# Token products in parts of 512, 512 and 128 instead of three of 384, in a hybrid encoder layer on one core

## The chip, the cores and the metric

One NeuronCore of a Trainium2 chip runs the whole step in one launch. The metric is device microseconds from the start to the end of an execution, as a median of several.

## The reference, cut to what matters

One inference step of one encoder layer with 1024 prompt tokens and 8 samples of 16 tokens (1152 tokens in all), model width 1024, everything in fp32:

```
z   = x @ w_in                     # 80 column tiles of 128, and 16 gate columns
o_A = chunk-band softmax attention (16 heads of 64; own chunk of 64 and 8 chunks before it)
o_B = gated DeltaNet (causal conv of 4, SiLU, delta rule by chunks, 8 heads of 128)
o_C = cross-attention into 256 memory tokens (4 heads of 256)
h   = LayerNorm(alpha * x + (sum_b sigmoid(gate_b) * o_b) @ w_out)
y   = LayerNorm(alpha * h + relu(h @ w_ff1 + b_ff1)^2 @ w_ff2 + b_ff2)
```

The outputs are y for prompt and samples, the new caches of keys and values of A and of the memory, and the states of the convolution and of the delta rule.

## The kernel before

Every wide product is made of three products in fp32r: each operand is split into a high and a low part, and high by high, high by low and low by high are added up in PSUM. `gemm` (line 183) walks the eight blocks of 128 input features. In each it issues three products, with `whi`, `whi` and `wlo` as the stationary operand and tokens as the moving one. Each product brings its own weight load.

A *unit* here is one tile of 128 output features over all 1152 tokens. `projected` (line 195) makes a unit in three parts of `CW` = 384 tokens. A part takes 24 products into one PSUM tile of the pair `ps` (tag g, two tiles), and is then handed to an evacuation function. The 1024 prompt tokens end 256 tokens into the third part; its last 128 tokens are the samples. There are 80 units of `w_in`, 32 of the first feed-forward matrix (line 1258), and a narrow one of 64 output columns for the gates of B (line 523).

The order of the stages is: A (attention, with the front of B woven in), C, B, output projection, feed-forward. In stage A, for each group g of two heads, the code makes q, k and v (`a_qk`, `a_v`), eight `a_prompt` units, `a_sample`, a gate unit and the three convolution units of `b_front`. A scheduler places the instructions on the queues of the engines by priorities and its own model. Each engine takes its queue strictly in order. DMAs are issued from the queue of SyncE (loads) and that of ScalarE (stores), in the same order as the other work there.

The tile `y` (two buffers of 384 columns in stage A) is shared: the evacuation of k copies a part of k into it and stores it (`o_akp`, lines 313 to 315, in the second and third part); the evacuation of v copies each part into it (line 338), stores it (`o_avp`) and lets TensorE transpose it (`pvt`); the convolution computes in it (lines 604 to 628), transposes it (`tp`) and stores it (`spq`, `spk`). A buffer is free again when its store has landed and its transposes are done.

`a_prompt` handles two query tiles of 128 against up to six key tiles. Four of them are used by both query tiles (256 moving columns). The two at the edges of the band are used by one query tile only; the other half of their 256 columns is zero, set once in `phase_a`.

`merge` (line 751) adds the gated branches up in DRAM (`og`), part by part. Stage B works on groups of three chunks of 128 tokens and keeps its 384.

Of the kernel before, what the change touches and what calls it, by code (L numbers as in the profile page):

```python
# [19 lines left out]
P = 128  # L20
D = 1024
SEQ = 1024
DB = 8
# [3 lines left out]
NCH = NT // CW  # L27
KT = D // P
# [35 lines left out]
class K:  # L64
# [158 lines left out]
    def load_x(self, pool):  # L223
        nc = self.nc
        xT = self.d["xT"].rearrange("c p (k n) -> c p k n", k=KT)
        self.first = [self.w_in(0)]
        for c in range(NCH):
            n = slice(c * CW, (c + 1) * CW)
            if c == 1:
                self.first.append(self.w_in(8))  # L230
            for k in range(KT):
                xr = pool.tile([P, (CW, 640, CW, 3 + CW)[k % 4]], F32, name=("e", "pt", "y", "z")[k % 4], bufs=2)[:, 0:CW]
                self.xlast = nc.sync.dma_start(xr, xT[c, :, k, :]).ins.name
                self.split(self.xh[:, k, n], self.xl[:, k, n], xr, "act")


    def phase_a(self, keep, pool, ps):
# [15 lines left out]
        for i in range(2):  # L253
            th = pool.tile([P, 6, 256], F32R, name=f"pth{i}")
            tl = pool.tile([P, 6, 256], F32R, name=f"ptl{i}")
            for t in (th, tl):
                nc.gpsimd.memset(t.bitcast(F32)[:, 4, 0:128], 0.0)
                nc.gpsimd.memset(t.bitcast(F32)[:, 5, 128:256], 0.0)
            A["pt"].append((th, tl))

        A["kl"] = [pool.tile([P, NT], F32R, name=f"kl{h}") for h in range(2)]
# [22 lines left out]
    def a_qk(self, g, pool):  # L284
        nc, d, A = self.nc, self.d, self.A

        qs = [pool.tile([P, NT], F32R, name=f"qs{h}") for h in range(2)]
        kd = [pool.tile([P, NT], F32R, name=f"kd{h}") for h in range(2)]
# [6 lines left out]
        def ev_q(c, p):  # L295
            n = slice(c * CW, (c + 1) * CW)
            for t, (r, o) in zip(qs, rows):
                nc.scalar.mul(t[r, n], p[r], 0.125)
                nc.vector.scalar_tensor_tensor(t[o, n], p[r], 0.125, t[r, n].bitcast(F32), op0=ALU.mult, op1=ALU.subtract)
            if c == 2:  # L300
                s = p[:, 256:384].rearrange("p (b i) -> p b i", b=DB)
                nc.scalar.mul(qb[0:64, :, 0:16], s[0:64], 0.125)
                nc.scalar.mul(qb[64:128, :, 16:32], s[64:128], 0.125)

        def ev_k(c, p):
            n = slice(c * CW, (c + 1) * CW)
# [4 lines left out]
            if c > 0:  # L311
                y = pool.tile([P, CW], F32, name="y", bufs=2)
                nc.scalar.copy(y, p)  # L313
                m = slice(128, 384) if c == 1 else slice(0, 256)
                nc.scalar.dma_start(d["o_akp"][g][:, (c - 1) * 256:c * 256], y[:, m])
            if c == 2:
                nc.gpsimd.tensor_copy(kr, y[:, 256:384])
# [11 lines left out]
    def a_v(self, g, pool, ps):  # L329
# [6 lines left out]
        def ev_v(c, p):  # L336
            vr = pool.tile([P, CW], F32, name="y", bufs=2)
            nc.scalar.copy(vr, p)
            if c == 1:
                nc.scalar.dma_start(d["o_avp"][g][:, 0:256], vr[:, 128:384])  # L340
            if c == 2:
                nc.scalar.dma_start(d["o_avp"][g][:, 256:512], vr[:, 0:256])
            pt = ps.tile([P, 512], F32, name="pvt", tag="f")
            for i in range(3):
                self.transpose(pt[:, i * P:(i + 1) * P], in_=vr[:, i * P:(i + 1) * P], identity=self.ident)
            m = 3 if c < 2 else 2
            src = pt[:, :m * P].rearrange("p (t h e) -> p t h e", t=m, h=2)
            dst = vv[:, 3 * c:3 * c + m]
            nc.scalar.copy(dst[:, :, :, 0:64], src)
            nc.vector.tensor_sub(dst[:, :, :, 64:128], src, dst[:, :, :, 0:64].bitcast(F32))  # L350
            if c == 2:
                nc.scalar.copy(vs, pt[:, 256:384])
# [20 lines left out]
    def a_prompt(self, g, G, h, pool, ps):  # L373
# [43 lines left out]
        e = 4 * 256 + P  # L417
        m = 256 if p0 >= 4 else P
        fh, fl = th.rearrange("p s q -> p (s q)"), tl.rearrange("p s q -> p (s q)")
        nc.scalar.copy(fh[:, e:e + m], tb[nb][:, :m])  # L420
        nc.vector.tensor_sub(fl[:, e:e + m], tb[nb][:, :m], fh[:, e:e + m].bitcast(F32))
# [76 lines left out]
    def b_setup(self, keep, pool, ps):  # L498
# [6 lines left out]
        z = pool.tile([P, CW], F32, name="e", bufs=2)  # L505
# [17 lines left out]
        for c in range(NCH):  # L523
            n = slice(c * CW, (c + 1) * CW)
            p = self.psg.tile([P, 512], F32, name="ps", tag="g")
            for k in range(KT):
                self.mm(p[0:64, :CW], lhsT=wh[:, k, :], rhs=self.xh[:, k, n], start=k == 0, stop=False)
                self.mm(p[0:64, :CW], lhsT=wh[:, k, :], rhs=self.xl[:, k, n], start=False, stop=False)
                self.mm(p[0:64, :CW], lhsT=wl[:, k, :], rhs=self.xh[:, k, n], start=False, stop=k == KT - 1)
            xa = pool.tile([P, CW], F32, name="e", bufs=2)[0:8]  # L530
            xb = pool.tile([P, CW], F32, name="e", bufs=2)[0:8]
            nc.scalar.activation(xa, p[0:8, :CW], AF.Identity, bias=par[:, 1:2])
# [7 lines left out]
            nc.scalar.activation(e, p[32:40, :CW], AF.Exp, scale=-1.0)  # L540
# [45 lines left out]
    def b_front(self, h, pool, ps):  # L586
# [3 lines left out]
        def conv(x, prev):  # L590
# [3 lines left out]
            def ev(c, p):  # L594
                n = slice(c * CW, (c + 1) * CW)
                z = pool.tile([P, 3 + CW], F32, name="z", bufs=2)
                nc.scalar.copy(z[:, 3:], p)
                if c == 0:
                    nc.gpsimd.memset(z[:, 0:3], 0.0)
                else:  # L600
                    nc.gpsimd.tensor_copy(z[:, 0:3], prev[0][:, CW:CW + 3])
                prev[0] = z
                y = pool.tile([P, CW], F32, name="y", bufs=2)
                nc.scalar.activation(y, p, AF.Copy, scale=wc[:, 3:4])  # L604
                w = CW if c < 2 else 256
                for i in range(3):
                    nc.vector.scalar_tensor_tensor(y[:, :w], z[:, i:i + w], wc[:, i:i + 1], y[:, :w], op0=ALU.mult, op1=ALU.add)  # L607
                if c == 2:
# [4 lines left out]
                    nc.gpsimd.tensor_copy(zs[:, :, 3:19], z[:, 259:387].rearrange("p (b i) -> p b i", b=DB))  # L613
                    ys = y[:, 256:384].rearrange("p (b i) -> p b i", b=DB)
# [3 lines left out]
                    nc.gpsimd.tensor_copy(co[:, 0, :], z[:, 256:259])  # L618
                    nc.gpsimd.tensor_copy(co[:, 1:9, :], zs[:, :, 16:19])
                    nc.scalar.dma_start(d["o_conv"][t], co.rearrange("p a i -> p (a i)"))  # L620
                e = pool.tile([P, CW], F32, name="e", bufs=2)
# [3 lines left out]
                for i in range(3):  # L625
                    self.transpose(tp[:, i * P:(i + 1) * P], in_=y[:, i * P:(i + 1) * P], identity=self.ident)
                if x < 2:
# [3 lines left out]
                    for i in range(3):  # L631
                        nc.scalar.activation(jk, tp[:, i * P:(i + 1) * P], AF.Square, accum_out=acc[:, h, 3 * c + i:3 * c + i + 1])
                if x > 0:
                    kn = pool.tile([P, CW], F32, name="kn", bufs=2)
                    nc.scalar.copy(kn, tp[:, :CW])
# [95 lines left out]
    def b_gate(self, a, t, pool, tags=("e", "oraw")):  # L731
# [4 lines left out]
        def ev(c, p):  # L736
            n = slice(c * CW, (c + 1) * CW)
            if a != 1:
                o = pool.tile([P, CW], F32, name=tags[1], bufs=2)
                nc.sync.dma_start(o, raw[t][:, n])  # L740
            e = pool.tile([P, CW], F32, name=tags[0], bufs=2)
# [3 lines left out]
            else:  # L745
                nc.vector.tensor_mul(e, e, o)
                self.merge(t, c, e, pool)
# [3 lines left out]
    def merge(self, t, c, e, pool):  # L751

        nc = self.nc
        dst = self.og[t][:, c * CW:(c + 1) * CW]
        if (t, c) in self.started:
            p = pool.tile([P, CW], F32, name="part", bufs=2)
            nc.sync.dma_start(p, dst)
            nc.gpsimd.tensor_add(e, e, p)
        self.started.add((t, c))
# [141 lines left out]
    def b_tail(self, h, c, pool, ps, o, gate, sample):  # L901
# [18 lines left out]
        self.merge(h, c, gate, pool)  # L920
# [121 lines left out]
    def c_q(self, h, pool):  # L1042
        nc, C = self.nc, self.C
        qh = pool.tile([P, 2, NT], F32R, name="qh", bufs=2)
        ql = pool.tile([P, 2, NT], F32R, name="ql", bufs=2)
        qz = C["qz"][h % 2]

        def ev_q(dt):
            def ev(c, p):
                n = slice(c * CW, (c + 1) * CW)  # L1050
                nc.scalar.mul(qh[:, dt, n], p, 0.0625)
                nc.vector.scalar_tensor_tensor(ql[:, dt, n], p, 0.0625, qh[:, dt, n].bitcast(F32), op0=ALU.mult, op1=ALU.subtract)
                if c == 2:
                    for a, b in self.spread2(qz[:, dt], p[:, 256:384]):
                        nc.scalar.mul(a, b, 0.0625)
# [127 lines left out]
    def out_early(self, po, pool):  # L1183
# [6 lines left out]
        for c in range(2):  # L1190
# [3 lines left out]
            for k in range(KT):  # L1194
                mg = pool.tile([P, CW], F32, name=("e", "oraw")[k % 2], bufs=2)
# [11 lines left out]
    def phase_out(self, pool, ps):  # L1207
# [36 lines left out]
        with self.pool("p2b") as pb:  # L1244
# [7 lines left out]
            for f0 in range(0, NF, blk):  # L1252
                hid = []
                for f in range(f0, f0 + blk):
# [3 lines left out]
                    for c in range(NCH):  # L1258
                        n = slice(c * CW, (c + 1) * CW)
# [145 lines left out]
```

## Time and profile before

| | |
|---|---|
| median of 3 runs | 2831.02 us (2816.75 to 2837.72) |
| profiled execution, whole | 2831.98 us |
| profiled execution, span from first to last instruction | 2830.2 us |
| mean granted clock of TensorE | 0.976 of full speed |
| TensorE products (PE), busy | 2685.3 us, 95% of the span, 16361 instructions |
| weight loads (PEld), busy | 2486.4 us, 88%, 16361 instructions |
| VectorE (DVE), busy | 1460.4 us, 52% |
| ScalarE (ACT), busy | 1008.4 us, 36% |
| GpSimd (POOL), busy | 819.5 us, 29% |

PE is the matmul side of TensorE, PEld its weight loads, which overlap. Products are pipelined: the duration of one is longer than the distance to the next, so the cost of a product in a stream is read from start to start, not from its duration. What lies outside the span is 1.8 us.

### The profile page before, as it was taken

How to read it: one execution, taken by the hardware profiler on the slowest of the kernel's cores; microseconds unless marked ns; L12 is line 12 of the kernel's file. 1: busy time of each engine (PE TensorE's matmuls, PEld its weight loads, DVE VectorE, ACT ScalarE, POOL GpSimd, SP SyncE). 2: the span in 40 equal slices, each digit the busy share in tenths (PEclk: the TensorE clock that was granted, in tenths of full speed). 3: DMA queues.
4: the chain of work that ended last, by engine and by line, in shares of the span. 5: the costliest groups of instructions: out<-in, count | busy, mean ns of one | idle time of the engine just before them, and what ended most of it. 6: DMA issues, size and time to landing. Idle time of an engine off the chain costs nothing.

```text
span 2830.2 us, 45047 instructions
## 1 busy us (share of the span) xinstructions
PE 2685.3 (95%) x16361; PEld 2486.4 (88%) x16361; DVE 1460.4 (52%) x3353; ACT 1008.4 (36%) x2749; POOL 819.5 (29%) x1197
## 2 busy tenths in 40 slices
PE   8989999989899989999989898999999999999997
PEld 7979899989899988998878888888989899998986
DVE  4646474737375655333366557554544444444445
ACT  4636363736364544222423333233411111111113
POOL 2222132212122221122355555432342121121212
PEclk9999999999999999999989999999999999999999
DMA  7252524333333424344676676654201011110101
GB/s 254 76 172 79 174 86 174 119 124 125 121 130 129 155 91 158 136 164 151 189 207 191 192 209 199 189 161 144 71 30 60 30 52 38 38 53 30 52 27 67
DMA packets 263006, 343.27 MB, mean 121 GB/s; under 512 B 54704, under 2 KB 178240, under 8 KB 258752
## 3 DMA queue, kind: packets, MB, share of 16 engines
q1 hardware_dynamic: 201344, 245.93, 27.7%
q10 hardware_dynamic: 61440, 94.46, 9.5%
q8 instruction: 129, 2.11, 0.3%
q14 instruction: 93, 0.76, 0.1%
HBM read 235.18 MB, written 105.13 MB: 120 GB/s over the span
## 4 chain that ended last, share of the span: by engine, by line
PE 51%; DMA 8%; DVE 4%; issue 3%; POOL 1%; ACT 1%; SPq 0%; DVEq 0%; ACTq 0%; POOLq 0%
PE ps L115 26%; PE op L115 15%; PE t L115 3%; PE S L115 1%; PE sc L115 1%; PE kk L115 1%; DMA wraw<-in_w_mem 1%; DVE tmp L775 1%; PE o L115 1%; PE tb L120 1%; DMA bv<-spn 1%; PE ob L115 1%; PE od L115 1%; DMA o_akp<-y 1%; DMA og<-gt 1%
## 5 line engine op out<-in xcount | busy, mean ns | idle before, releaser
L115 PE MATMUL ps<-xh,whi 128*128 128x384 f32 x2712 | 958.1, 353 | 31.4 <-ACT y L313 13.9
L115 PE MATMUL ps<-xl,whi 128*128 128x384 f32 x2712 | 935.6, 345 | 0.0
L115 PE MATMUL ps<-xh,wlo 128*128 128x384 f32 x2712 | 933.5, 344 | 0.9 <-DVE wlo L169 0.9
L115 PEld LDWEIGHTS ps<-xh,whi 128*128 128x128 f32 x2712 | 517.7, 191 | 50.3 <-ACT y L313 14.5
L115 PEld LDWEIGHTS ps<-xl,whi 128*128 128x128 f32 x2712 | 517.4, 191 | 14.1 <-issue 2.9
L115 PEld LDWEIGHTS ps<-xh,wlo 128*128 128x128 f32 x2712 | 515.9, 190 | 10.2 <-issue 3.9
L168 POOL TENSOR_SCALAR whi<-wraw 128x512 fp32r<-128x512 f32 x261 | 180.6, 692 | 513.6 <-PE ps L115 414.8
L1289 DVE TENSOR_TENSOR acc<-op,acc 128x512 f32<-128x512 f32 x252 | 174.2, 691 | 276.1 <-PE op L115 276.0
L1263 ACT ACTIVATE r<-ps,bf 128x384 f32<-128x384 f32 x96 | 55.7, 581 | 664.7 <-PE ps L115 664.7
L169 DVE TENSOR_TENSOR wlo<-wraw,whi 128x512 fp32r<-128x512 f32 x261 | 195.2, 748 | 185.0 <-POOL whi L168 179.0
L115 PE MATMUL op<-h,uh 128*128 128x512 f32 x576 | 225.6, 392 | 1.2 <-DVE sm L1293 1.2
L115 PE MATMUL op<-h,ul 128*128 128x512 f32 x576 | 226.1, 392 | 0.0
L115 PE MATMUL op<-l,uh 128*128 128x512 f32 x576 | 225.5, 392 | 0.0
L371 POOL TENSOR_SCALAR pt<-pt,sta 128x640 f32<-128x640 f32 (+3 forms) x144 | 114.1, 793 | 293.5 <-DVE sta L370 242.5
L168 POOL TENSOR_SCALAR uh<-r 128x384 fp32r<-128x384 f32 x96 | 55.5, 578 | 492.0 <-ACT r L1264 480.1
L367 DVE CUSTOM_DVE_ANT_0 pt<-S,tab 128x640 f32<-128x640 f32 (+4 forms) x128 | 83.9, 656 | 122.8 <-PE S L115 85.6
L607 DVE SCALAR_TENSOR_TENSOR y<-z,wc,y 128x384 f32<-128x384 f32 (+1 forms) x216 | 128.7, 596 | 17.5 <-ACT y L604 15.5
L115 PEld LDWEIGHTS op<-h,ul 128*128 128x128 f32 x576 | 108.2, 188 | 23.9
L115 PEld LDWEIGHTS op<-h,uh 128*128 128x128 f32 x576 | 108.2, 188 | 19.5 <-DVE sm L1293 2.0
L115 PEld LDWEIGHTS op<-l,uh 128*128 128x128 f32 x576 | 108.1, 188 | 15.5
L369 ACT ACTIVATE pt<-pt,sta 128x640 f32<-128x640 f32 (+3 forms) x144 | 101.4, 705 | 49.4 <-DVE sta L368 35.7
L169 DVE TENSOR_TENSOR ul<-r,uh 128x384 fp32r<-128x384 f32 x96 | 53.7, 560 | 102.2 <-POOL uh L168 102.2
(374 smaller groups left out, 4600.5 us busy)
## 6 DMA issues: line engine op xcount, KB each, us to landing
wraw<-in_w_in SPq DMA_DIRECT2D x160, 256.0 KB
kb<-in_cak SPq DMA_DIRECT2D x16, 1024.0 KB
vb<-in_cav SPq DMA_DIRECT2D x16, 1024.0 KB
o_aks<-kb ACTq DMA_DIRECT2D x16, 1024.0 KB
wraw<-in_w_ff SPq DMA_DIRECT2D x64, 256.0 KB
w2raw<-in_w_ff SPq DMA_DIRECT2D x64, 256.0 KB
o_avs<-vb ACTq DMA_DIRECT2D x16, 992.0 KB
spn<-kn ACTq DMA_DIRECT2D x48, 192.0 KB
```

The costliest lines, as they stand in the source:

```text
L115: ins = self.nc.tensor.matmul(out, **kw)
L120: ins = self.nc.tensor.transpose(out, **kw)
L168: nc.gpsimd.tensor_scalar(hi, raw, 1.0, 0.0, op0=ALU.mult, op1=ALU.add)
L169: nc.vector.tensor_sub(lo, raw, hi.bitcast(F32))
L367: nc.vector.tensor_tensor_reduce(out=P_, in0=S, in1=tab, scale=1.0, scalar=-3e38, op0=ALU.add, op1=ALU.max, accum_out=st[:, 0:1])
L369: nc.scalar.activation(P_, P_, AF.Exp, bias=st[:, 1:2], accum_out=st[:, 2:3])
L371: nc.gpsimd.tensor_scalar(P_, P_, st[:, 3:4], 0.0, op0=ALU.mult, op1=ALU.add)
L607: nc.vector.scalar_tensor_tensor(y[:, :w], z[:, i:i + w], wc[:, i:i + 1], y[:, :w], op0=ALU.mult, op1=ALU.add)
L775: nc.vector.tensor_tensor(tmp[:, 0:t, 0:t], y[:, 0:t, 0:t], m[:, 0:t, t].unsqueeze(1).broadcast_to([72, t, t]), op=ALU.mult)
L1263: nc.scalar.activation(r, p[:, :CW], AF.Relu, bias=bf[:, f:f + 1])
L1289: nc.vector.tensor_add(a, o, a)
```

## The change

Tokens are cut into `CH` = (0, 512), (512, 1024), (1024, 1152): the halves of the prompt, and the samples. The units of `w_in`, the first feed-forward matrix, the gate columns of B, and the loading of x go by these parts. What evacuates a part knows now that the third part holds the samples alone, so q and k write only the sample tiles there, the convolution takes its prompt steps in two parts and the samples alone in the third, and k is stored once per unit (512 columns, from part two) instead of twice. The store of v is one too. `y` is 512 columns wide with three buffers in stage A. Tiles that only need the prompt shrink from 1152 to 1024 columns. In `a_prompt` the edge tiles are used at 128 columns, without the zero halves. `xT` lies in DRAM as (8, 128, 1152).

```
+CH = ((0, 512), (512, 1024), (1024, 1152))
...
-        for c in range(NCH):
-            ps = self.psg.tile([P, 512], F32, name="ps", tag="g")
-            for k in self.gemm(ps[:, :CW], w, self.xh, self.xl, c * CW, (c + 1) * CW):
+        for c, (n0, n1) in enumerate(CH):
+            ps = self.psg.tile([P, 512], F32, name="ps", tag="g")[:, :n1 - n0]
+            for k in self.gemm(ps, w, self.xh, self.xl, n0, n1):
                 yield
-            evac(c, ps[:, :CW])
+            evac(c, ps)
...
         def ev_k(c, p):
+            if c == 2:
+                nc.scalar.copy(kr, p)
+                return
...
-            if c > 0:
-                y = pool.tile([P, CW], F32, name="y", bufs=2)
+            if c == 1:
+                y = pool.tile([P, 512], F32, name="y", bufs=3)
                 nc.scalar.copy(y, p)
-                m = slice(128, 384) if c == 1 else slice(0, 256)
-                nc.scalar.dma_start(d["o_akp"][g][:, (c - 1) * 256:c * 256], y[:, m])
+                nc.scalar.dma_start(d["o_akp"][g], y)
...
         def ev_v(c, p):
-            vr = pool.tile([P, CW], F32, name="y", bufs=2)
+            m = (4, 4, 1)[c]
+            vr = pool.tile([P, 512], F32, name="y", bufs=3)[:, :m * P]
             nc.scalar.copy(vr, p)
             if c == 1:
-                nc.scalar.dma_start(d["o_avp"][g][:, 0:256], vr[:, 128:384])
-            if c == 2:
-                nc.scalar.dma_start(d["o_avp"][g][:, 256:512], vr[:, 0:256])
+                nc.scalar.dma_start(d["o_avp"][g], vr)
...
-        use = [(s, k) for s, k in enumerate(full)] + [(4, p1)] + ([(5, p0 - 4)] if p0 >= 4 else [])
-        for n, (s, k) in enumerate(use):
-            self.mm(o, lhsT=vv[:, k, h, :], rhs=th[:, s, :], start=n == 0, stop=False)
-            self.mm(o, lhsT=vv[:, k, h, :], rhs=tl[:, s, :], start=False, stop=n == len(use) - 1)
+        every, second, first = slice(0, 256), slice(P, 256), slice(0, P)
+        use = [(s, k, every, every) for s, k in enumerate(full)] + [(4, p1, first, second)] + ([(4, p0 - 4, second, first)] if p0 >= 4 else [])
+        for n, (s, k, a, b) in enumerate(use):
+            self.mm(o[:, b], lhsT=vv[:, k, h, :], rhs=th[:, s, a], start=n == 0, stop=False)
+            self.mm(o[:, b], lhsT=vv[:, k, h, :], rhs=tl[:, s, a], start=False, stop=n == len(use) - 1)
...
-                    for c in range(NCH):
-                        n = slice(c * CW, (c + 1) * CW)
-                        p = self.psg.tile([P, 512], F32, name="ps", tag="g")
-                        run(self.gemm(p[:, :CW], w, hh, hl, c * CW, (c + 1) * CW))
-                        r = pb.tile([P, CW], F32, name="r", bufs=2)
+                    for n0, n1 in CH:
+                        n = slice(n0, n1)
+                        p = self.psg.tile([P, 512], F32, name="ps", tag="g")[:, :n1 - n0]
+                        run(self.gemm(p, w, hh, hl, n0, n1))
+                        r = pb.tile([P, 512], F32, name="r", bufs=2)[:, :n1 - n0]
```

## Rows read from the trace of the kernel before

**Rows 1.** Windows of A, B, feed-forward: length; busy PE, PEld, DVE, ACT, POOL; clock; DMA.

```profile
0.00:1110.00 1110.00, 1038.35 (x6768) 989.70 (x6769) 628.21 (x1673) 583.33 (x1596) 273.62 (x524) 0.97 0.39 133
...
1460.00:1960.00 500.00, 461.21 (x3132) 419.35 (x3132) 293.33 (x792) 153.74 (x560) 230.42 (x271) 0.95 0.64 188
...
2020.00:2830.00 810.00, 794.92 (x3980) 721.34 (x3978) 369.99 (x548) 125.45 (x231) 188.67 (x234) 0.99 0.14 46
```

**Rows 2.** Waits of TensorE's products in stage A: us in total, times, longest.

```profile
PE pvt L120 <- ACT y L338: 32.6, 6, 8.8
PE ps L115 <- ACT y L313: 13.9, 3, 7.1
```

**Rows 3.** Waits of ScalarE in stage A, same columns.

```profile
ACT y L338 <- DMA o_akp<-y: 72.8, 9, 12.4
...
ACT y L313 <- DMA o_avs<-vb: 13.7, 2, 9.0
```

**Rows 4.** Timeline of ScalarE and its DMA queue, group 1 of stage A: start, duration.

```profile
186.26 0.34 ACTq L315 DMA_DIRECT2D o_akp<-y  x1
...
201.22 0.48 ACT L338 COPY y<-ps 128x384 f32<-128x384 f32 x1 [12.40 <-DMA o_akp<-y]
```

**Rows 5.** Windows of six stretches at reduced clock in stage A: the first, and the sum.

```profile
201.70:206.30 4.60, 4.55 (x16) 4.55 (x17) 0.56 (x1) 0.96 (x2) 0.00 (x0) 0.50 0.52 193
...
sum 35.20, PE 27.88 PEld 27.70 DVE 8.80 ACT 12.32 POOL 1.48; mean PE 4.65 PEld 4.62 DVE 1.47 ACT 2.05 POOL 0.25
```

**Rows 6.** Products by shape: count, busy us, mean ns, idle before them.

```profile
L115 PE MATMUL ps<-xh,whi 128*128 128x384 f32 x2688 | 950.0, 353 | 31.4 <-ACT y L313 13.9 <-POOL whi L168 7.6 <-ACT y L338 3.6
```

**Rows 7.** Timeline of products in the feed-forward stage: 384 and 512 columns in streams.

```profile
2310.15 0.34 PE L115 MATMUL ps<-xh,whi 128*128 128x384 f32 x1
...
2311.56 0.39 PE L115 MATMUL op<-h,uh 128*128 128x512 f32 x1
...
2312.94 0.34 PE L115 MATMUL ps<-xh,wlo 128*128 128x384 f32 x1
```

**Rows 8.** Timeline of products, output projection: a stream of 512 columns without other shapes.

```profile
2000.02 0.39 PE L115 MATMUL op<-woh,xl 128*128 128x512 f32 x1
...
2003.20 0.40 PE L115 MATMUL op<-wol,xh 128*128 128x512 f32 x1
```

**Rows 9.** Timeline of products, early output projection at the end of stage B.

```profile
1925.17 0.39 PE L115 MATMUL ps<-wlo,xh 128*128 128x512 f32 x1
...
1928.91 0.40 PE L115 MATMUL ps<-hi,xl 128*128 128x512 f32 x1
```

**Rows 10.** Timeline of products and weight loads: two fp32r products of 128 columns.

```profile
213.34 0.22 PE L115 MATMUL S<-kd,qs 128*128 128x128 f32 x1
...
213.40 0.28 PE L115 MATMUL S<-kl,qs 128*128 128x128 f32 x1
213.45 0.19 PEld L115 LDWEIGHTS ps<-xh,whi 128*128 128x128 f32 x1
213.51 0.39 PE L115 MATMUL ps<-xh,whi 128*128 128x384 f32 x1
213.56 0.19 PEld L115 LDWEIGHTS ps<-xl,whi 128*128 128x128 f32 x1
```

**Rows 11.** Timeline of products: transposes of 128 columns in a stream.

```profile
831.35 0.60 PE L120 MATMUL tb<-cst,pt 128*128 128x128 f32 x4
831.78 0.27 PE L120 MATMUL od<-cst,pt 128*128 128x128 f32 x1
```

**Rows 12.** Groups of ScalarE in stage A by shape: the same copy at two widths.

```profile
L415 ACT CAST pth<-tb 128x512 fp32r<-128x512 f32 x80 | 44.2, 592 | 16.8 <-PE tb L120 10.6 <-DMA kb<-in_cak 5.7
...
L415 ACT CAST pth<-tb 128x256 fp32r<-128x256 f32 x32 | 12.1, 378 | 21.8 <-DMA o_avs<-vs 18.5 <-PE tb L120 3.2
```

**Rows 13.** Timeline of ScalarE: the evacuation of one part of k.

```profile
713.17 0.48 ACT L308 CAST kd<-ps 64x384 fp32r<-64x384 f32 x1 [0.25 <-PE ps L115]
...
715.55 0.48 ACT L313 COPY y<-ps 128x384 f32<-128x384 f32 x1 [0.63 <-DVE kl L309]
```

More of the change, by code (lines that the diff above doesn't have):

```diff
@@ L253, in phase_a @@
         for i in range(2):
[L254 to L261, printed above, removed]
+            A["pt"].append(tuple(pool.tile([P, 5, 256], F32R, name=f"{n}{i}") for n in ("pth", "ptl")))
+        A["kl"] = [pool.tile([P, SEQ], F32R, name=f"kl{h}") for h in range(2)]
         for h in range(2):
@@ L285, in a_qk @@
         nc, d, A = self.nc, self.d, self.A
-        qs = [pool.tile([P, NT], F32R, name=f"qs{h}") for h in range(2)]
-        kd = [pool.tile([P, NT], F32R, name=f"kd{h}") for h in range(2)]
+        qs = [pool.tile([P, SEQ], F32R, name=f"qs{h}") for h in range(2)]
+        kd = [pool.tile([P, SEQ], F32R, name=f"kd{h}") for h in range(2)]
         kl = A["kl"]
@@ L336, in ev_v @@
         def ev_v(c, p):
-            vr = pool.tile([P, CW], F32, name="y", bufs=2)
+            m = (4, 4, 1)[c]
+            vr = pool.tile([P, 512], F32, name="y", bufs=3)[:, :m * P]
             nc.scalar.copy(vr, p)
             if c == 1:
-                nc.scalar.dma_start(d["o_avp"][g][:, 0:256], vr[:, 128:384])
-            if c == 2:
-                nc.scalar.dma_start(d["o_avp"][g][:, 256:512], vr[:, 0:256])
-            pt = ps.tile([P, 512], F32, name="pvt", tag="f")
-            for i in range(3):
-                self.transpose(pt[:, i * P:(i + 1) * P], in_=vr[:, i * P:(i + 1) * P], identity=self.ident)
[L346 to L352, printed above, removed]
+                nc.scalar.dma_start(d["o_avp"][g], vr)
+            pt = ps.tile([P, 512], F32, name="pvt", tag="f")[:, :m * P]
+            for i in range(m):
+                self.transpose(pt[:, i * P:(i + 1) * P], in_=vr[:, i * P:(i + 1) * P], identity=self.ident)
+            if c < 2:
+                src = pt.rearrange("p (t h e) -> p t h e", t=m, h=2)
+                dst = vv[:, 4 * c:4 * c + 4]
+                nc.scalar.copy(dst[:, :, :, 0:64], src)
+                nc.vector.tensor_sub(dst[:, :, :, 64:128], src, dst[:, :, :, 0:64].bitcast(F32))
+            else:
+                nc.scalar.copy(vs, pt)
                 dv = d["o_avs"][g][124:128]
@@ L504, in b_setup @@
         self.after_x(nc.sync.dma_start(B["ng"], d["norm_g"]))
-        z = pool.tile([P, CW], F32, name="e", bufs=2)
+        z = pool.tile([P, 512], F32, name="e", bufs=2)[:, :CW]
         nc.gpsimd.memset(z, 0.0)
@@ L522, in b_setup @@
         nc.gpsimd.memset(gbt[0:64], 0.0)
-        for c in range(NCH):
-            n = slice(c * CW, (c + 1) * CW)
+        for n0, n1 in CH:
+            n, w = slice(n0, n1), n1 - n0
             p = self.psg.tile([P, 512], F32, name="ps", tag="g")
             for k in range(KT):
[L527 to L532, printed above, removed]
+                self.mm(p[0:64, :w], lhsT=wh[:, k, :], rhs=self.xh[:, k, n], start=k == 0, stop=False)
+                self.mm(p[0:64, :w], lhsT=wh[:, k, :], rhs=self.xl[:, k, n], start=False, stop=False)
+                self.mm(p[0:64, :w], lhsT=wl[:, k, :], rhs=self.xh[:, k, n], start=False, stop=k == KT - 1)
+            xa = pool.tile([P, 512], F32, name="e", bufs=2)[0:8, :w]
+            xb = pool.tile([P, 512], F32, name="e", bufs=2)[0:8, :w]
+            nc.scalar.activation(xa, p[0:8, :w], AF.Identity, bias=par[:, 1:2])
             nc.scalar.activation(xb, xa, AF.Abs)
@@ L594, in ev @@
             def ev(c, p):
[L595 to L599, printed above, removed]
-                else:
[L601 to L608, printed above, removed]
+                n, m = slice(*CH[c]), (4, 4, 1)[c]
+                w = m * P
+                y = pool.tile([P, 512], F32, name="y", bufs=3)[:, :w]
+                nc.scalar.activation(y, p, AF.Copy, scale=wc[:, 3:4])
+                if c < 2:
+                    z = pool.tile([P, 515], F32, name="z", bufs=2)
+                    nc.scalar.copy(z[:, 3:], p)
+                    if c == 0:
+                        nc.gpsimd.memset(z[:, 0:3], 0.0)
+                    else:
+                        nc.gpsimd.tensor_copy(z[:, 0:3], prev[0][:, 512:515])
+                    prev[0] = z
+                    for i in range(3):
+                        nc.vector.scalar_tensor_tensor(y, z[:, i:i + w], wc[:, i:i + 1], y, op0=ALU.mult, op1=ALU.add)
+                else:
                     zs = pool.tile([P, DB, 19], F32, name="zs", bufs=1)
@@ L624, in ev @@
                 tp = ps.tile([P, 512], F32, name="tp", tag="f")
-                for i in range(3):
+                for i in range(m):
                     self.transpose(tp[:, i * P:(i + 1) * P], in_=y[:, i * P:(i + 1) * P], identity=self.ident)
@@ L630, in ev @@
                     jk = pool.tile([P, P], F32, name="jk", bufs=1)
-                    for i in range(3):
-                        nc.scalar.activation(jk, tp[:, i * P:(i + 1) * P], AF.Square, accum_out=acc[:, h, 3 * c + i:3 * c + i + 1])
+                    for i in range(m):
+                        nc.scalar.activation(jk, tp[:, i * P:(i + 1) * P], AF.Square, accum_out=acc[:, h, 4 * c + i:4 * c + i + 1])
                 if x > 0:
-                    kn = pool.tile([P, CW], F32, name="kn", bufs=2)
-                    nc.scalar.copy(kn, tp[:, :CW])
+                    kn = pool.tile([P, 512], F32, name="kn", bufs=2)[:, :w]
+                    nc.scalar.copy(kn, tp[:, :w])
                     nc.scalar.dma_start(self.spn[x - 1][h][:, n], kn)
@@ L736, in ev @@
         def ev(c, p):
-            n = slice(c * CW, (c + 1) * CW)
+            n, w = slice(*CH[c]), CH[c][1] - CH[c][0]
             if a != 1:
-                o = pool.tile([P, CW], F32, name=tags[1], bufs=2)
+                o = pool.tile([P, 512], F32, name=tags[1], bufs=3 if tags[1] == "y" else 2)[:, :w]
                 nc.sync.dma_start(o, raw[t][:, n])
-            e = pool.tile([P, CW], F32, name=tags[0], bufs=2)
+            e = pool.tile([P, 512], F32, name=tags[0], bufs=2)[:, :w]
             self.sigmoid(e, p, e)
@@ L746, in ev, with merge @@
                 nc.vector.tensor_mul(e, e, o)
-                self.merge(t, c, e, pool)
+                self.merge(t, n, e, pool)
         yield from self.projected(w + t, ev)
-    def merge(self, t, c, e, pool):
+    def merge(self, t, n, e, pool):
         nc = self.nc
-        dst = self.og[t][:, c * CW:(c + 1) * CW]
-        if (t, c) in self.started:
-            p = pool.tile([P, CW], F32, name="part", bufs=2)
+        dst = self.og[t][:, n]
+        units = {(t, u) for u in range(n.start // P, n.stop // P)}
+        assert units <= self.started or not units & self.started
+        if units <= self.started:
+            p = pool.tile([P, 512], F32, name="part", bufs=2)[:, :n.stop - n.start]
             nc.sync.dma_start(p, dst)
             nc.gpsimd.tensor_add(e, e, p)
-        self.started.add((t, c))
+        self.started |= units
         nc.scalar.dma_start(dst, e)
@@ L1043, in c_q @@
         nc, C = self.nc, self.C
-        qh = pool.tile([P, 2, NT], F32R, name="qh", bufs=2)
-        ql = pool.tile([P, 2, NT], F32R, name="ql", bufs=2)
+        qh = pool.tile([P, 2, SEQ], F32R, name="qh", bufs=2)
+        ql = pool.tile([P, 2, SEQ], F32R, name="ql", bufs=2)
         qz = C["qz"][h % 2]
```

57 lines of the change are left out of this document (28 added, 29 removed).

## The prediction, made before the changed kernel ran

> **What bounds the kernel now.** I read the windows by stage first [rows 1]. The products keep TensorE busy for 1038 of 1110 us in stage A, for 461 of 500 us in B and for 795 of 810 us in the feed-forward stage, while VectorE and ScalarE are busy for 57% and 53% even in A. So a product that grows dearer is paid for nearly everywhere; only A and B have idle time that could be won, 72 and 39 us.
>
> Next, what TensorE waits for in A [rows 2]. 32.6 us of its idle time, in six pieces, stand before the transposes of v and end with ScalarE's copy of v into `y`; 13.9 us in three pieces end with the copy of k into `y`. ScalarE's own waits [rows 3] say why. The copies of v waited 72.8 us in nine pieces for stores of k (`o_akp`) that read the two buffers of `y`. In group 1 the copy begins 15.0 us after the later of these stores was issued [rows 4]. The copies of k are another matter: the wait ahead of them ends with `o_avs<-vb`, a store that sits in ScalarE's queue until its `vb` has been loaded. The third `y` does nothing for that.
>
> These waits cost twice. After them the granted clock is 0.50 of full speed, the lower of its levels of 1.2 and 2.4 GHz; before the first of the stretches TensorE had stood idle for 8.8 us [rows 2, 5]. In the six stretches that follow the waits for `o_akp`, 27.9 us of products run at half speed, which loses 13.9 us. Together the store of k costs 32.6 + 13.9 = 46.5 us.
>
> Last, the price of a product in a stream, start to start [rows 7 to 11], since durations overlap. From 2310.15 to 2311.56 stand eight products of 384 columns: 0.176 us each. From there to 2312.94 stand six of 512: 0.230 us each. A stream of 512 alone is 14 steps in 3.18 us, 0.227 us each [rows 8], and one in the same `ps` tiles, during B, 16 steps in 3.74 us, 0.234 us each [rows 9].
>
> **The price of a part of 128 columns.** This decides the case. By columns, 512 + 512 + 128 is as much as three times 384. But every product brings a weight load, and a short product no longer covers it. The trace holds fp32r products of 128 columns, in pairs [rows 10]. The second starts 0.06 us after the first, which looks like a price by columns. But the weight load for the product behind it starts at 213.45, the next one at 213.56, 0.11 us later, and the product that starts at 213.51 lasts 0.39 us instead of the usual 0.34 [rows 7]: it was let in early and then waited 0.05 us for its weights. Transposes of 128 columns, one load each, come every 0.11 us over four steps [rows 11]. So I take 0.110 us, bounded by 0.06 below (the recorded start to start) and 0.11 above.
>
> The Trainium skill, TensorE: Matmul & The Clock Gate, section "LDWEIGHTS (loading the stationary operand)", gives a load as its columns over 1.2 per ns, that is 107 ns for 128 columns. By that rule, the trace agrees (0.11 us), and a sum made with it would be 8 us lower than mine.
>
> **The change, part by part.**
> 1. Products of the units. There are 112 full units (2688 products of each kind over 24) [rows 6]. A unit costs 72 x 0.1765 = 12.71 us before, and 48 x 0.230 + 24 x 0.110 = 11.04 + 2.64 = 13.68 us after: +0.97 us, in all +108.6 us. Of it 32 units or 31 us lie in the feed-forward stage, where nothing else can hide it (2% idle); 57 in A (55 us), 10 in C, 13 in B. With 0.227 or 0.234 for 512 columns the sum is +93 or +130 us. The narrow unit of B's gates is left out; its weights have 64 columns.
> 2. Edge tiles. 192 products go from 256 to 128 columns. 256 columns cost about 256/384 x 0.176 = 0.118 us, 128 cost 0.110: -1.4 us. By columns alone it would be -11 us.
> 3. Third `y` and one store of k. Parts one and two of v now take buffers that no store of k holds; part three takes that of k. It needs it 2.64 + 11.04/2 x 2 + 2.64 = 16.3 us of products after part two of k ended, less the 2.9 us that k's evacuation takes until its store [rows 13], so 13.4 us after the issue; 15.0 us went by in group 1 [rows 4]. So a wait of some 2 us can remain where no attention work lies between. If it does, behind it in ScalarE's queue are the exponentials of `a_prompt` and the evacuation of the convolution, and TensorE waits for these. I take 80% of the 46.5 us: -37 us. The bounds are 0 (the one store of 256 KB lands later than two of 128 KB, and part three waits as long as part one did) and -60 (the 13.9 us before the copies of k go too, because the order moves).
> 4. Evacuation against PSUM. `ps` has two tiles. The next unit's first part can begin when part two is out of its tile, and only part three lies between: 2.64 us where there were 24 x 0.176 = 4.2 us. A copy gains (592 - 378)/256 = 0.84 ns per column [rows 12], so 0.11 us from 384 to 512. The chain of k has five such steps and took 2.9 us [rows 13]; it becomes 3.4 us, 0.8 us too long, in 8 units: 6 us, half of it covered by attention products: +3 us. Bounds: 0, and 1 us in all 57 units of A, +57 us, since ScalarE is half busy with other work and comes late.
> 5. Stage B. The fill steps of 8 per part become 0.69 us (0.33 in part three) instead of 0.53 us, so the recurrence waits up to 0.16 us longer behind one. B is idle for 8% [rows 1], so of its 12.6 us I let 1 us fall into idle time: -1 us. At the ends none of it does, or all of it.
> 6. At nothing: fewer steps of q, k and convolution on ScalarE and VectorE (idle over 40% in A, so their time isn't on the path; if they were, a step less in 24 convolution units is worth under 10 us), zeros not set, and the load of x, which has as many pieces and bytes and differs in the first part alone (2 us either way).
>
> Sum against the profiled execution of 2832.0 us (2830.2 us of span and 1.8 us around it; 1 us above the median, so no correction): 2832.0 + 108.6 - 1.4 - 37 + 3 - 1 = **2904 us**, 2.6% slower.
>
> **The rivals.**
> First, a part of 128 costs its columns alone, because loads run ahead of short products. For it: the 0.06 us of [rows 10]. Against it: the product that then took 0.05 us longer, and [rows 11]. A unit would cost 11.04 + 24 x 0.06 = 12.48 us, -0.23 us; 112 units -26 us. Time: 2832 - 26 - 1.4 - 37 - 1 = 2767 us, faster by 2.3%. It decides from the price at which 112 units cost what the rest gives: (37 + 1.4 - 2)/112 = 0.33 us per unit, so (12.71 + 0.33 - 11.04)/24 = 0.083 us per product of 128. The same page of the Trainium skill, section "Back-to-back issue gap", speaks for this side: its gap for a product by itself, columns over 2.4 per ns plus 2.5 ns, makes the unit as dear after as before, and its figure for load and product in pairs, 81 ns for 128 columns (for another type), lies at the point where it tips.
>
> Second, the gain in A is whole and the products are at their cheap end: 0.227 us, and both kinds of wait in [rows 2] go. 2832 + 93 - 1.4 - 60 - 13 = 2850 us, 0.6% slower, no difference. For it: A has no other large waits. Against it: the waits for `o_avs<-vb` don't touch `y`.
>
> Third, the wait moves instead of going: part three of v waits for the store of k as part one did, and PSUM is late in A. 2832 + 108.6 - 1.4 + 20 = 2959 us. For it: the store is as slow as before, ScalarE issues it from the same queue behind the same 1 MB stores. Against it: one more buffer gives 11 us.
>
> **How the numbers follow.** Forecast (2855 to 2950 us) 0.60; first rival 0.06; second 0.17 (within 1%); third and worse 0.16; 0.01 for what I don't see. A measurement of this kernel can tell a change of about 1% from none (its three runs spread by 0.7%). Faster by over 1%: 0.07, the first rival and the unseen; within 1%: 0.17, the second; slower by over 1%: 0.76, the forecast and the third. The range for 8 in 10 leaves out the first rival and the far end of the third: 2842 to 2960 us.
>
> **What would show it.** In the timeline of the feed-forward stage products of 128 columns should come every 0.11 us and the stage should grow by 31 us, to some 841 us; 0.06 us there would prove the first rival. In A, waits of `pvt` for the copies of v should fall from 32.6 us to under 8 us with the stretches of half clock behind them; if new waits of `ps` for evacuations stand there, step 4 was too small. The prediction would be wrong if A won more than the 72 us that it now idles, or if 512 columns were dearer than 0.234 us under the traffic of A.

## The result and the profile after

The changed kernel takes 2964.55 us (median of 4, 2959.29 to 2973.12) against 2826.96 us before: a ratio of 1.0489, 95% interval 1.044 to 1.0538, 4.9% slower. Its profiled execution took 2959.3 us with a span of 2957.5 us, 127.3 us more than the one before. I forecast slower, but by 72 us, so the sum fell 55 us short of the profiled execution, and the time of the median lies just above the range.

Where the 127.3 us lie can be read from the first and last starts of products that only one stage has: the last `od` ends stage A, the first `kk` begins B, the last `ot` ends it.

| us | before | after | difference |
|---|---|---|---|
| A, to the last `od` | 1112.4 | 1173.8 | +61.4 |
| C, to the first `kk` | 279.5 | 287.5 | +8.0 |
| B, to the last `ot` | 520.2 | 541.2 | +21.0 |
| output and feed-forward, to the end of the span | 918.1 | 955.0 | +36.9 |

The windows of the changed kernel for A, B and the feed-forward stage (columns as in [rows 1]) say the same in another way: the share of time in which TensorE is busy is as before, so what was added is busy time.

```profile
0.00:1174.00 1174.00, 1108.48 (x6809) 929.92 (x6809) 609.23 (x1562) 567.72 (x1558) 262.52 (x444) 0.97 0.38 126
...
1461.00:2002.00 541.00, 499.43 (x3248) 438.72 (x3247) 306.44 (x842) 172.53 (x609) 256.69 (x312) 0.92 0.64 188
...
2129.00:2957.00 828.00, 813.22 (x3893) 675.46 (x3891) 372.75 (x536) 122.01 (x225) 199.24 (x223) 0.99 0.12 42
```

In A it idles for 65.5 us, before for 72 [rows 1], and its mean granted clock is 0.97 as before. If the third `y` had done what I expected of it, some 26 us of idling would have gone there.

The timeline of the changed kernel's feed-forward stage gives the prices, start to start.

```profile
2309.03 0.39 PE L117 MATMUL op<-h,uh 128*128 128x512 f32 x1
...
2310.84 0.40 PE L117 MATMUL op<-h,ul 128*128 128x512 f32 x1
2311.07 0.40 PE L117 MATMUL ps<-xh,whi 128*128 128x512 f32 x1
...
2313.42 0.39 PE L117 MATMUL ps<-xl,whi 128*128 128x512 f32 x1
...
2336.77 0.28 PE L117 MATMUL ps<-xl,whi 128*128 128x128 f32 x1
...
2339.22 0.28 PE L117 MATMUL ps<-xh,wlo 128*128 128x128 f32 x1
```

Ten products of 512 columns into `ps` take 2.35 us, 0.235 us each; eight into `op`, just before, take 1.81 us, 0.226 us each. The 22 products of 128 columns take 2.45 us: 0.111 us each, not the 0.06 of their columns. That is the step of the loads in [rows 10, 11]. By the Trainium skill, TensorE: Matmul & The Clock Gate, section "LDWEIGHTS (loading the stationary operand)", a load of 128 columns of weights would take 107 ns, an estimate by its formula; the 0.111 us agree with it.

That it is the load, and not a least time that any product takes, one unit of the same kernel shows: the narrow one of B's gates, whose weights have 64 columns. Its third part has the same 128 moving columns, and the granted clock over it is 1.00.

```profile
53.55 0.23 PE L117 MATMUL ps<-xl,whi 128*64 128x128 f32 x1
...
54.87 0.22 PE L117 MATMUL ps<-xh,wlo 128*64 128x128 f32 x1
```

These are 22 steps in 1.32 us, 0.060 us each: half the weights, and the price of 128 moving columns is their columns again.

Now the waits of TensorE in A (first three lines) and those of ScalarE there (last two), which answer to [rows 2] and [rows 3].

```profile
PE pvt L122 <- DVE vv L346: 29.8, 6, 6.5
PE od L117 <- DVE sta L364: 11.0, 1, 11.0
...
PE ps L117 <- ACT y L313: 3.6, 4, 1.4
...
ACT vv L345 <- DMA vb<-in_cav: 47.4, 4, 12.4
...
ACT vv L345 <- DMA o_avs<-vb: 25.3, 2, 13.6
```

The waits for `o_akp` are gone, and the transposes of v wait about as long as before, 29.8 us instead of 32.6, six times. Only the thing waited for is another: ScalarE's copies behind them stand for 47.4 + 25.3 = 72.7 us before the load of `vb` and the store `o_avs` that reads it, where they stood for 72.8 us before `o_akp` [rows 3]. The timeline of all engines in group 2 shows it.

```profile
347.54 0.33 SPq L439 DMA_DIRECT2D vb<-in_cav  x1
...
353.56 0.60 PE L122 MATMUL pvt<-cst,y 128*128 128x128 f32 x4
...
362.28 0.28 ACTq L445 DMA_DIRECT2D o_avs<-vb  x1
...
363.03 0.59 ACT L345 CAST vv<-pvt 128x512 fp32r<-128x512 f32 x1 [13.56 <-DMA o_avs<-vb]
...
364.49 1.08 PE L122 MATMUL pvt<-cst,y 128*128 128x128 f32 x4 [6.50 <-DVE vv L346]
```

The first part of v found its `y` and was transposed at 353.56, so the wait for `y` is gone. But then ScalarE's next work, the copy of that transpose out of PSUM, stands behind a store in ScalarE's own queue: `o_avs` from `vb`, whose load was issued at 347.54. The store could be issued at 362.28. Until then the one PSUM tile of `pvt` stays full and the next transposes wait.

The kernel before has both waits at the same time in its group 2 (timeline of all engines there).

```profile
325.45 0.33 SPq L443 DMA_DIRECT2D vb<-in_cav  x1
...
339.06 0.48 ACT L338 COPY y<-ps 128x384 f32<-128x384 f32 x1 [12.28 <-DMA o_akp<-y]
...
340.01 0.29 ACTq L449 DMA_DIRECT2D o_avs<-vb  x1
```

The store stood right behind the copy that waited for `o_akp`, and went out 14.6 us after its load was issued, as in the changed kernel (14.7 us). So I take it that without the wait for `y` ScalarE would have come to this store and waited there instead. That is argued from these rows; the runs with another source for the store try it below.

### The profile page after: what moved, and what is told of

Same layout as the page of the kernel before. It is cut to its first block, busy times and chain, and to the rows that moved or that the text cites. A ratio compares the mean times of both kernels' runs of the same rounds, so it can differ in the third digit from the quotient of the medians.

```text
span 2957.5 us, 44732 instructions
## 1 busy us (share of the span) xinstructions
PE 2826.4 (96%) x16361; PEld 2381.8 (81%) x16361; DVE 1444.9 (49%) x3233; ACT 991.4 (34%) x2701; POOL 822.3 (28%) x1117
## 4 chain that ended last, share of the span: by engine, by line
PE 77%; DMA 13%; DVE 4%; issue 3%; POOL 1%; ACT 1%; SPq 0%; ACTq 0%; DVEq 0%; POOLq 0%
PE ps L117 46%; PE op L117 15%; DMA vb<-in_cav 4%; PE S L117 3%; PE t L117 3%; PE od L117 3%; PE tb L122 2%; PE sc L117 1%; DMA bv<-spn 1%; PE kk L117 1%; PE tp L122 1%; PE o L117 1%; DMA kb<-in_cak 1%; DMA wraw<-in_w_mem 1%; PE ob L117 1%
## 5 line engine op out<-in xcount | busy, mean ns | idle before, releaser
L117 PE MATMUL ps<-xh,whi 128*128 128x512 f32 (+1 forms) x2712 | 998.3, 368 | 16.3 <-ACT xh L166 7.5
L117 PE MATMUL ps<-xh,wlo 128*128 128x512 f32 (+1 forms) x2712 | 984.5, 363 | 0.0
L117 PE MATMUL ps<-xl,whi 128*128 128x512 f32 (+1 forms) x2712 | 982.4, 362 | 0.0
L117 PEld LDWEIGHTS ps<-xh,wlo 128*128 128x128 f32 x2712 | 522.7, 193 | 83.8 <-issue 4.9
L170 POOL TENSOR_SCALAR whi<-wraw 128x512 fp32r<-128x512 f32 x261 | 192.8, 740 | 542.5 <-PE ps L117 452.2
L1263 ACT ACTIVATE r<-ps,bf 128x512 f32<-128x512 f32 (+1 forms) x96 | 55.8, 581 | 698.9 <-PE ps L117 698.9
L171 DVE TENSOR_TENSOR wlo<-wraw,whi 128x512 fp32r<-128x512 f32 x261 | 205.2, 791 | 157.4 <-POOL whi L170 153.9
L170 POOL TENSOR_SCALAR uh<-r 128x512 fp32r<-128x512 f32 (+1 forms) x96 | 62.7, 653 | 512.7 <-ACT r L1264 509.2
L604 DVE SCALAR_TENSOR_TENSOR y<-z,wc,y 128x512 f32<-128x512 f32 x144 | 111.9, 777 | 20.4 <-ACT z L597 15.9
L171 DVE TENSOR_TENSOR ul<-r,uh 128x512 fp32r<-128x512 f32 (+1 forms) x96 | 60.3, 629 | 98.8 <-POOL uh L170 98.8
```

Of the source, the lines that this page charges most:

```text
L117: ins = self.nc.tensor.matmul(out, **kw)
L170: nc.gpsimd.tensor_scalar(hi, raw, 1.0, 0.0, op0=ALU.mult, op1=ALU.add)
L171: nc.vector.tensor_sub(lo, raw, hi.bitcast(F32))
L604: nc.vector.scalar_tensor_tensor(y, z[:, i:i + w], wc[:, i:i + 1], y, op0=ALU.mult, op1=ALU.add)
L1263: nc.scalar.activation(r, p, AF.Relu, bias=bf[:, f:f + 1])
```

## The experiments

Theory P: the loss is the price of the products, of which the weight loads behind short ones are the core. Theory Q: the third `y` brings nothing because the store `o_avs`, which waits for the load of `vb` in ScalarE's queue, lies behind the wait for `y`. Theory S, the rival of P: the loss comes from waits and the new order. Each result stands against the kernel before, run on the same chip; ratios are with their 95% intervals.

**The new parts in the feed-forward stage alone.**

```
-                    for c in range(NCH):
-                        n = slice(c * CW, (c + 1) * CW)
+                    for n0, n1 in ((0, 512), (512, 1024), (1024, 1152)):
+                        n = slice(n0, n1)
```

> The kernel before, with the new parts (512, 512, 128) in the feed-forward stage alone; its columns were 384 three times. Theory P (the loss is the price of the products: about 0.234 us for 512 columns, 0.111 for 128, against 0.1765 for 384) expects 48 x 0.234 + 24 x 0.111 - 72 x 0.1765 = 1.19 us more for each of 32 units: +38 us, all of it in this stage. Theory S (the loss comes from the waits and the new order in stages A and B, the products cost no more than 0.97 us per unit as predicted or less) expects +31 us or less; by columns alone it would be about -7 us.

2869.73 against 2827.09 us, ratio 1.0147 (1.012 to 1.0174): +43 us. In the profiled executions the stretch behind the last `ot` grew from 918.1 to 955.4 us, and nothing else changed by over 2 us. P holds. This stage has no waits to speak of, so S has nothing here to work with; the run says nothing on S in A and B.

**The old parts back in the feed-forward stage of the changed kernel** (the same edit reversed).

> The changed kernel with three parts of 384 back in the feed-forward stage alone. Theory P (products) expects about -37 to -42 us against the changed kernel, the mirror of the run with the new parts there alone (some 2925 us). Theory S expects the same saving here or less, at most -31 us.

2930.44 against 2832.03 us, ratio 1.0346 (1.0328 to 1.0365): 34 us under the changed kernel by the medians, some 40 by the two ratios. The medians lie between what P and S expected; the stretch behind the last `ot` shrank by 38.6 us, to 916.4, as P has it. Stage B, whose code is the same in both, was 559.1 us long instead of 541.2 in these two executions.

**Parts of 512, 320, 320, and of 512, 512, 64, 64, in the feed-forward stage of the kernel before.** The same edit with other bounds.

> The kernel before with parts of 512, 320 and 320 columns in the feed-forward stage alone. Theory P in its narrow form (only a product too short to cover the next weight load costs extra) expects 0.234 + 2 x 0.147 = 0.528 us against 3 x 0.1765 = 0.5295 us per step: -4 to +4 us. If wide products or uneven parts as such were dear, +15 us or more.

> The kernel before with parts of 512, 512, 64 and 64 columns in the feed-forward stage alone: the same columns as 512, 512, 128, with 24 weight loads more in each of 32 units. Theory P expects a product of 64 columns to cost what one of 128 does, 0.111 us: 24 x 0.111 x 32 = 85 us more than the run with 512, 512, 128 there (which took 42 us more than the kernel before), so +120 to +130 us. If the third part were dear by its columns, as much as that run: +35 to +50 us.

The first: 2830.42 against 2826.73 us, ratio 1.0004 (0.9982 to 1.0026), no difference. Parts of 512 are not dear as such, and uneven parts cost nothing at 320 columns, whose products come every 0.147 us (ten steps in 1.47 us):

```profile
2316.37 0.31 PE L115 MATMUL ps<-xl,whi 128*128 128x320 f32 x1
...
2317.84 0.31 PE L115 MATMUL ps<-xh,wlo 128*128 128x320 f32 x1
```

The second: 2962.74 us, ratio 1.0478 (1.0427 to 1.053), +136 us, above the 120 to 130 expected, for the same columns and 24 products more per unit. Here are its products of 64 columns in the timeline.

```profile
2322.07 0.28 PE L115 MATMUL ps<-xh,whi 128*128 128x64 f32 x1
...
2323.30 0.28 PE L115 MATMUL ps<-xh,wlo 128*128 128x64 f32 x1
```

Eleven steps in 1.23 us are 0.112 us each: half the columns, the same price. The step from 512, 512, 128 to this, 136 - 43 = 93 us, is 0.121 us for each of 768 added products; P expected 85. This settles P: a third part is not dear by its columns, which are the same, but by the number of its products. With the gate unit above, where weights half as wide halve the price of 128 columns, the weight load is what a short product costs.

**The edge tiles alone** (the edit of `a_prompt` in the kernel before).

> The kernel before with the edge tiles of the band at 128 columns alone. The prediction's step has 192 products at 0.110 instead of 0.118 us: -1.4 us; by columns -11 us. Theory P expects the first: no difference that can be measured, -3 to +3 us, unless the changed order moves waits of stage A (up to 10 us either way).

2832.93 against 2826.73 us, ratio 1.0019 (0.9996 to 1.0042): no gain, as the load's price says; by columns it would have been -11 us. The waits in A moved all the same: those of the transposes of v grew from 32.6 to 55.3 us, those for the copy of k (13.9 us) went.

**The third `y` with parts of 384,** in the kernel before, with the edge tiles, whose smaller tiles make room for it.

```
-            vr = pool.tile([P, CW], F32, name="y", bufs=2)
+            vr = pool.tile([P, CW], F32, name="y", bufs=3)
```

> The kernel before, with the third tile y (of 384 columns) and the edge tiles at 128 columns, which make room for it; parts stay at 384 and the store of k stays in two. The theory of the prediction (the copies of v wait for y alone) expects -37 us, with the edge tiles -38. Theory Q (behind the wait for y stands the store o_avs, which blocks ScalarE's queue until its load of vb has landed, so another tile y only shows that wait) expects -10 to +5 us, and that the products before the transposes of v still idle for 20 to 40 us in stage A in all, with ScalarE waiting for vb or o_avs.

2838.9 against 2827.09 us, ratio 1.004 (1.0024 to 1.0056): 12 us slower. The third tile gives nothing here. Its waits in stage A, TensorE's and then ScalarE's:

```profile
PE ps L115 <- ACT e L218: 33.2, 6, 6.2
...
ACT pth L410 <- DMA o_avs<-vs: 48.9, 4, 12.8
ACT y L333 <- DMA o_akp<-y: 47.1, 6, 8.5
```

TensorE waits 33.2 us for another evacuation. This run is not quite step 3: k is still stored in two pieces, which hold two of the three tiles, and the copies of v still wait 47.1 us for `o_akp`. And the store that ScalarE now stands before is not the one from `vb` that Q named, but the eight small stores of the new values (`o_avs` from `vs`), issued in a row:

```profile
747.12 12.50 ACTq L350 DMA_DIRECT2D o_avs<-vs  x8
```

They take 9 to 13 us in seven of the eight groups, 5 to 8 us in the kernel before. Why they take longer is open. So the run is slower than even Q's -10 to +5 us, and the waits are only in part those that Q named; step 3 itself is tried by the next run and by the changed kernel.

**Two tiles `y` in the changed kernel** (every `bufs=3` of `y` back to 2).

> The changed kernel with two tiles y instead of three. The theory of the prediction (a third y is worth 37 us) expects +30 us or more against the changed kernel, some 2995 us. Theory Q (while o_avs blocks ScalarE's queue, a third y shows little; and k is stored once instead of twice) expects -10 to +15 us.

2972.17 us, ratio 1.0507 (1.0485 to 1.0529): 8 us over the changed kernel, whose own four runs reach that far, and within what Q expected. In the profiled executions stage A is not longer with two tiles, 1171.5 us against 1173.8; what this one has more lies in B. So the third `y`, on which step 3 put 37 us, shows no worth in A. Here step 3 falls.

**The store that waits, taken from the input.** The old values that `o_avs` stores lie in DRAM already; a store from there waits for no load. First without a place in the order, with two tiles `y` and then with three and the edge tiles:

```
-            nc.scalar.dma_start(d["o_avs"][g][0:124, bs, :], vb[4:128].rearrange("p b s e -> p b (s e)"))
+            self.after_x(nc.scalar.dma_start(d["o_avs"][g][0:124, bs, :], d["cav"][g][4:128, bs, :]))
```

> The kernel before, with the store of the old values of A (o_avs) read from the input in DRAM instead of the tile vb, so that it waits for no load in ScalarE's queue; two tiles y as before, the bytes stored are the same. Theory Q (both waits lie on top of each other) expects that this alone leaves the waits for o_akp: the 13.9 us ahead of the copies of k go with their half-clock stretches, -15 to -25 us. The theory of the prediction expects -14 to -20 us as well; the two part in the run with both edits.

> Both edits in the kernel before: a third y (with the edge tiles at 128 columns) and o_avs stored from the input in DRAM; parts stay at 384. Theory Q expects that only both together free the queue: -45 to -70 us, most of the 50 us that the products idled ahead of copies into y and of the half-clock stretches behind it. The theory of the prediction expects -37 from y and some -15 from the store, each also when alone. If neither holds (another load or store takes their place), -20 us or less.

2883.3 us, ratio 1.02 (1.0176 to 1.0223), and 2884.4 us, ratio 1.0203 (1.0184 to 1.0222). All expectations missed, and the windows of the first show why: its first 200 us, and from 300 to 1100 us.

```profile
0.00:200.00 200.00, 80.00 (x375) 70.94 (x375) 35.88 (x87) 36.24 (x78) 18.82 (x45) 0.74 0.44 160
300.00:1100.00 800.00, 797.74 (x5410) 768.44 (x5409) 482.59 (x1296) 449.57 (x1242) 213.62 (x403) 1.00 0.37 124
```

With nothing to wait for, the scheduler placed all sixteen stores of 1 MB in the first 200 us, where TensorE then idles for 120 of 200 us; in ScalarE's queue such an issue took 7.4 us in the median, against 0.29 us for the store from `vb` before. After that stage A runs at full clock and TensorE idles for 2 us in 800, with two tiles `y` and parts of 384. So the waits in A belong to these stores and loads, not to `y`. The runs that follow hold each store to its place behind the score products of its half group:

```
+            ins = nc.scalar.dma_start(d["o_avs"][g][0:124, bs, :], d["cav"][g][4:128, bs, :])
+            self.tc.add_manual_dep(ins.ins, self.last, mybir.DependencyInfo(
+                mybir.DependencyClass.NoSync, mybir.DependencyReason.DATA), reason="in place")
```

> The kernel before, o_avs stored from the input in DRAM, and held to its place in the order (after the score products of the same half group), which the earlier run without that lost: there all sixteen stores were issued in the first 200 us and the rest of stage A then ran nearly without waits. Two tiles y, parts of 384. Theory Q (the store that waits for vb in ScalarE's queue, and the store of k that lands late behind it, lie on top of each other) expects -10 to -30 us, with the waits for o_akp still there. If the store of k landed late only because of the stores that waited, all of it goes: -45 to -70 us.

> As the run before it, with the third tile y and the edge tiles at 128 columns; parts of 384. Theory Q expects -45 to -70 us against the kernel before, where the third y alone gave +12. If some other load or store takes their place, -20 us or less.

> The changed kernel (parts 512, 512, 128, three tiles y) with o_avs stored from the input in DRAM and held to its place. Theory Q expects that the gain which the third y should have brought appears now: -35 to -60 us against the changed kernel, so some 2905 to 2930 us, near the time that was predicted. If the waits ahead of the transposes of v have another cause, within 15 us of the changed kernel.

In the kernel before: 2812.22 against 2832.03 us, ratio 0.9935 (0.992 to 0.995), -20 us. With the third `y` and the edge tiles too: 2796.34 us, ratio 0.9873 (0.9852 to 0.9893), -36 us, less than the -45 to -70 expected but faster than both kernels of this case. In the changed kernel: 2922.7 us, ratio 1.0331 (1.0298 to 1.0363), 42 us under the changed kernel, as Q expected. The third `y` with the edge tiles, which made the kernel 12 us slower, gives 16 us once the queue is free. What waits then, in A, in these three in turn:

```profile
PE S L115 <- DMA kb<-in_cak: 41.5, 8, 6.9
...
ACT y L338 <- PE ps L115: 47.0, 18, 3.8
```

```profile
PE S L115 <- DMA kb<-in_cak: 30.4, 8, 7.7
```

```profile
PE S L117 <- DMA kb<-in_cak: 17.3, 7, 3.2
```

No copy of v waits for a store any more, even with two tiles `y`, so I was wrong in Q as well: I had expected the waits for `o_akp` to stay there. They went with the store that waited. Why `o_akp` had landed late was not tried by itself. TensorE now waits for the load of the old keys, `kb`, which has one tile; that is the next thing in this stage, and part of the expected gain went there.

The last and the second of these three, 2922.7 and 2796.3 us, differ by the parts and what came with them (one store of k, the wider tiles). The 126 us would be 1.13 us for each of 112 units, but they do not lie so. In the profiled executions, which are 118.3 us apart, A is longer by 45.0 us, C by 6.8, B by 31.8 and the rest by 34.7. The feed-forward stage pays 1.08 us a unit, as before; A pays 0.79, so there the other edits win back some 20 us once the queue is free; and B pays 2.4.

## Why the prediction was wrong, point by point

*What bounds the kernel.* Right: TensorE nearly everywhere, so what its products grew by arrives. Stage A idles for 65.5 us where it idled for 72, and the feed-forward stage takes its 37 us in full.

*Step 1, the products.* Right in mechanism, too small in size. 0.110 us for 128 columns measured 0.111. For 512 I had three rows, 0.227, 0.230 and 0.234, and took the middle one; it measured 0.235 in the units, the row of the same `ps` tiles [rows 9]. That should have been the choice, being the nearest form. The term of +108.6 us for 112 units would be 129 us by the feed-forward stage (36.9 us over 32 units, 1.15 us each, times 112). This is some 20 of the 55 us by which the sum fell short.

*Step 2, the edge tiles.* Right: no gain that can be measured.

*Step 3, the third `y`.* This is the step that failed, with some 30 us. The term was -37 us; stage A grew by 61.4 us where 57 units cost 57 x 1.15 = 66 us, so all the other edits of this stage together gave some 4 us, if its units cost what those of the feed-forward stage do. I had named `o_avs` as a wait of its own that the third `y` would not touch, and priced it only at the three places where the profile put it down to that store. But ScalarE takes its queue in order, as group 2 shows. In four of the seven groups after the first the store came behind the wait for `y`, as at 340.01 above; in the other three it had gone out ahead of k's last copy, which waited for it (5.3, 9.0 and 4.7 us) and stored late. And the profile names the wait that ended last. That the wait moves was my third rival, though it had the new wait in the wrong place: in the third part of v and its store of k, not in front of the copy out of `pvt`. That its 2959 us came out is luck: it added 20 us in A, which did not come, to products that it had 20 us too cheap.

*Step 4, evacuation against PSUM.* Small, as I had it (+3 us), but no loss shows: the waits of `ps` for evacuations in A came to 5.1 us after the change (3.6 of them for the copy of k), to 22.1 before, 13.9 of them for the copy of k [rows 2].

*Step 5, stage B.* Wrong in sign and too small. I had 12.6 us for 13 units less 1; at 1.15 us the units cost 15, and B grew by 21.0. The other three runs with the changed kernel's B show more: 552.2 to 559.1 us, against 514.3 to 528.1 in the ten kept runs with the old parts there (520.2 in the kernel before). So the parts cost B 13 to 45 us, 34 in the mean, and its 541.2 us in the changed kernel's profile are the shortest of four. It is not idle time of TensorE, 41.6 to 52.9 us in the four and 46.8 to 53.2 in the ten, but busy time, and the mean granted clock in B is lower: 0.91 to 0.92 in the four, 0.94 to 0.97 in the ten. Why it falls was not tried. So S has a share here, some 20 us beyond the products.

Of the 55 us by which the sum fell short, some 31 are then step 3, 20 the products and 7 stage B, less 3 in C, whose ten units cost 8.0 us.

*The rivals.* The first (columns alone, 0.06 us) is refuted by the 0.111 us of the products and by the parts of 64; its price holds only where the weights have 64 columns. The second needed the gain in A that was not there.

## What to carry to other kernels

In the streams of this case a product costs the larger of its columns and its weight load, so widths are chosen so that no part falls under the load: 320, 384 and 512 columns are equal by the column (0.147, 0.1765 and 0.235 us), and a leftover part of 128 costs nearly twice its columns (0.111 against 0.060 us), in every unit. And a buffer that a store holds is worth another one only after asking what stands behind the same wait in the same queue: put the engine's queue in order and price the wait that would end next, not the one that the profile names. A store that is freed from its dependency should be given a place in the order when its dependency is taken away.

## What the runs showed that I had not expected

Products of 512 columns differ in price within one stage and at one clock: in the streams above 0.235 us when they go to `ps` from the first feed-forward matrix, 0.226 us when they go to `op` from the second. Over a longer stretch (2300 to 2600 us) the steps average 0.235 and 0.229 us, which over 48 products in 112 units would be worth some 30 us, an estimate. It was not tried which of the operands, or the work of the other engines at that time, makes it.

Stores without any dependency were moved ahead by the scheduler, the last of them by 0.8 ms (issued at 165.8 us instead of 992.1), where they made the kernel 56 us slower than before; the same bytes in their place are 71 us cheaper (2883 against 2812 us), and 88 us with three tiles `y` (2884 against 2796).
